# First key and value weights requested beside the feature tile that uses them, and modulation rows of 128 columns instead of 256

## The chip, the cores and the metric

One core of one Trainium2 chip runs the whole program. The metric is the device time of one execution in microseconds. The profile names the engines PE (TensorE: the matmuls), PEld (its weight loads), DVE (VectorE), ACT (ScalarE), POOL (GpSimd) and SP (SyncE, whose queue here issues all DMAs).

## What is computed

Two layers of a diffusion backbone over 1024 latent tokens and 256 context tokens, 1024 features wide. Each layer modulates its input with a per-feature shift and scale, projects it to queries, keys, values and a gate, attends, projects back, and ends in a LayerNorm. The change lies in the opening of the first layer, which is this part of the reference:

```python
shift, scale, gate = jnp.split(silu_c @ w_ada[i] + b_ada[i], 3, axis=-1)          # latent tokens
shift_c, scale_c, gate_c = jnp.split(silu_cc @ w_ada[i] + b_ada[i], 3, axis=-1)   # context tokens
u = h * (1.0 + scale[:, None, :]) + shift[:, None, :]
uc = hc * (1.0 + scale_c) + shift_c
...
q, k, v, g = _split_a(u @ w_in)      # 1024 queries, 256 keys, 256 values, 1024 gates
```

The rest of the first layer is windowed attention with four key and value heads, that of the second a neighbourhood attention. Neither is touched.

## The kernel before

Features lie on the 128 partitions: the input is eight feature tiles (`kt` = 0 to 7) of 128 features by 1280 tokens, cut into three chunks of 512, 512 and 256 tokens. Keys and values of the first layer need the sum over all eight feature tiles, and the kernel builds them while the tiles arrive. For each `kt` it does this:

- `mod_load`: two requests for the modulation weights (`wada`, 512 KB each, the halves `hf` of the contracted dimension) and one for the input tile (`hraw`, 640 KB). `Weights.load(n)` requests the first n of eight key and value weight pieces (`wr`, 256 KB each; pieces 0, 1, 4, 5 are keys, 2, 3, 6, 7 values; key pieces serve four feature tiles, value pieces two).
- `mod_rows` (line 503): matmuls of the 32-column `sil` (SiLU of the conditioning; two of its 32 columns are used) with `wada`, into four strips of 32 partitions of the PSUM tile `kc`, and a copy of the strips to SBUF by ACT (`rows`, line 505). Each strip holds a partial sum over a quarter of the features, for 256 columns: 128 of shift, 128 of scale.
- `mod` (line 512): a matmul of `rows` with the 0/1 matrix `sel` adds the four partial sums and turns them into columns, and DVE adds the bias (`adc`, line 513).
- `u_make` (lines 527 to 532): ACT scales and shifts chunk 0, DVE chunks 1 and 2; ACT rounds to a high part `uAh`, DVE subtracts for a low part `uAl`.
- `Weights.split(n)`: the same high and low split for weight pieces: ACT's cast (line 160, `wh` for keys, `wv` for values), DVE's subtraction (line 162).
- `k_mm` (lines 541 to 543): 12 matmuls of 512 columns into four key accumulators (`kp`), and six of 256 columns into `kc`. `v_mm` (lines 551 to 553): 12 matmuls of 256 columns into `vps`.

So a chain runs from `wada`'s landing through line 503, the copy, line 512, `adc` and `u_make` to the key and value matmuls of the same tile. The matmuls named `warm` and `vps<-zero` (line 446) compute nothing that is kept.

The code states the work per tile in a loop; a scheduler then fixes the order on each engine, and each engine runs its own list in that order, waiting on semaphores. SP issues its requests in order too, and the list of SP has eight semaphores in turn, so a request waits until the one eight places ahead has landed. A request into a buffer also waits until the buffer's last reader is done: `wr` has four buffers in this stage, `hraw` four, and `wada` shares ten with the split value weights. Since `kc` is one tile, the six key matmuls into it wait for the ACT copy out of it. The stage ends at the first matmul named `pv`, line 240, the values of the remaining tokens.

Of the kernel before, what the change touches and what calls it, by code (L numbers as in the profile page):

```python
# [11 lines left out]
F32 = mybir.dt.float32  # L12
# [7 lines left out]
P = 128  # L20
# [60 lines left out]
def build(tc, i, out):  # L81
    nc = tc.nc
    mm = nc.tensor.matmul
# [3 lines left out]
    def pool(name, side="left", **kw):  # L87
        st = ExitStack()
        p = st.enter_context(tc.tile_pool(name=name, bufs=1, side=side, reuse_waits="tile", **kw))
        return p, st  # L90
# [4 lines left out]
    def psbig(name):  # L95
        return ps.tile([P, 1024], F32, tag="big", bufs=2, name=name)
# [4 lines left out]
    cp = es.enter_context(tc.tile_pool(name="cp", bufs=1, side="left"))  # L101
    ident = cp.tile([P, P], F32, name="ident")
    cT = cp.tile([P, KT, 2], F32, name="cT")
    dma(cT, i["cT"])
    bad = cp.tile([P, 50], F32, name="bad")
    dma(bad, i["bada"])
    sel = bad[:, 48:50]
    lnc = cp.tile([P, 2, KT], F32, name="lnc")
    half = cp.tile([P, 1], F32, name="half")
    nc.vector.memset(half, -0.5)  # L110
# [75 lines left out]
    w = Weights(srcs)  # L186
# [247 lines left out]
    pp, pp_st = pool("p0", "right")  # L434
# [3 lines left out]
    sil = pp.tile([P, KT, 32], F32, name="sil")  # L438
# [5 lines left out]
    def warm(out, n):  # L444
        for _ in range(n):
            mm(out, zero[:, 0:P], zero, start=True, stop=True)
# [40 lines left out]
    kc = psbig("kc")  # L487
    vps = psbig("vps")
    raws, wada, rows = {}, {}, {}

    def mod_load(kt):
        wada[kt] = [pp.tile([P, 4, 2 * P], F32, tag="wada", bufs=10, name="wada") for _ in range(2)]
        for hf in range(2):
            dma(wada[kt][hf], i["wadaC"][kt, hf])
        raws[kt] = pp.tile([P, T], F32, tag="hraw", bufs=4, name="hraw")
        dma(raws[kt], i["hT"][:, kt, :])

    def mod_rows(kt):

        for hf, wt in enumerate(wada.pop(kt)):  # L500
            for g in range(4):
                gs = slice(32 * g, 32 * g + 32)
                mm(kc[gs, 512:768], sil[:, 4 * hf + g, :], wt[:, g, :], start=hf == 0, stop=hf == 1, tile_position=(0, 32 * g))
        rows[kt] = pp.tile([P, 2 * P], F32, tag="rows", bufs=2, name="rows")
        nc.scalar.copy(rows[kt], kc[:, 512:768])

    def mod(kt):

        r = rows.pop(kt)
        pa = kc[:, 768 + 4 * kt : 772 + 4 * kt]  # L510
        for x in range(2):
            mm(pa[:, 2 * x : 2 * x + 2], r[:, x * P : (x + 1) * P], sel, start=True, stop=True)
        nc.vector.tensor_tensor(
            adc[:, kt],
            pa.rearrange("p (x v) -> p x v", x=2),
            bad[:, kt : kt + 9 : 8].unsqueeze(2).to_broadcast([P, 2, 2]),
            ALU.add,
        )

    def u_make(kt):  # L520
        r = raws.pop(kt)
        for c, (t0, n) in enumerate(CHUNKS):
            v, tok = c // 2, slice(t0, t0 + n)
            x = r[:, tok]
            sc, sh = adc[:, kt, 1, v : v + 1], adc[:, kt, 0, v : v + 1]
            if c == 0:
                nc.scalar.activation(x, x, AF.Identity, bias=sh, scale=sc)
            else:
                nc.vector.tensor_scalar(x, x, sc, sh, ALU.mult, ALU.add)
            hi, lo = uA.at(kt, tok)  # L530
            nc.scalar.copy(hi, x)
            nc.vector.tensor_tensor(lo, x, f32(hi), ALU.subtract)

    def k_mm(kt):
        for c, (t0, n) in enumerate(CHUNKS):
            for nt in range(2):
                hi, lo = w.got[KEYS[2 * (kt // 4) + nt]]
                sl = slice((kt % 4) * P, (kt % 4 + 1) * P)
                rh, rl = uA.at(kt, slice(t0, t0 + n))
                pt = kps[c, nt] if c < 2 else kc[:, nt * C : nt * C + C]  # L540
                mm(pt, hi[:, sl], rh, start=kt == 0 and (c < 2 or nt == 0), stop=False)
                mm(pt, lo[:, sl], rh, start=False, stop=False)
                mm(pt, hi[:, sl], rl, start=False, stop=kt == KT - 1 and (c < 2 or nt == 1))

    def v_mm(kt):
        hi, lo = w.got[VALUES[kt // 2]]
        sl = slice((kt % 2) * 256, (kt % 2 + 1) * 256)
        for t in range(4):
            lh, ll = uA.at(kt, slice(t * P, (t + 1) * P))
            pt = vps[:, t * 256 : (t + 1) * 256]  # L550
            mm(pt, lh, hi[:, sl], start=kt == 0 and t % 2 == 0, stop=False)
            mm(pt, lh, lo[:, sl], start=False, stop=False)
            mm(pt, ll, hi[:, sl], start=False, stop=kt == KT - 1 and t % 2 == 1)


    upto = (3, 4, 6, 7, 8)
    for kt in range(-1, KT + 1):
        if kt + 1 < KT:
            for n in range(3) if kt < 0 else (kt + 3,) if kt + 3 < KT else ():
                mod_load(n)  # L560
                w.load(upto[min(n, 4)])
            mod_rows(kt + 1)
        if kt > 0:
            k_mm(kt - 1)
        if kt + 1 < KT:
            mod(kt + 1)
        if kt < 0:

            warm(vps[:, 0:512], 8)
        if kt > 0:  # L570
            v_mm(kt - 1)
        if kt < KT and kt >= 0:
            u_make(kt)
            w.split(upto[min(kt, 4)])
    dma(ident, i["ident"])
    dma(lnc, i["lnc"])
    dma(cos, i["cos"])
# [224 lines left out]
    for p in range(8):  # L802
# [6 lines left out]
        if p < 7:  # L809
            n = len(att)  # L810
# [72 lines left out]
    for b in range(10):  # L883
# [14 lines left out]
        g = gts[:, b // 8]  # L898
# [229 lines left out]
    for n, row in enumerate(rowsB):  # L1128
        ex = []
        if n < len(subsB):  # L1130
            h, jp, r = subsB[n]
# [55 lines left out]
    for b in range(8):  # L1187
        x = ob.tile([P, D], F32, tag="x", bufs=2, name="x")
# [130 lines left out]
```

## Time and profile before

| | |
|---|---|
| times of three runs | 1464.61, 1461.41 and 1463.99 us, median 1463.99 |
| profiled execution | 1466.38 us, of which the span is 1464.6 us |
| mean granted clock of TensorE over the span | 0.992 |
| TensorE busy | 1399.2 us, 96% of the span |
| stage of the change | from the start to the first `pv` matmul at 72.92 us |

A row of the timeline gives the start in us, the length, the engine, line, operation, tiles and the number of instructions merged into the row; in square brackets stands the idle time of that engine before it, and whose work ended it. Several rows of TensorE overlap, since a matmul starts while the one ahead is still flowing through the array; from one start to the next is what a matmul costs. A row of the table by windows gives the stretch, its length, for PE, PEld, DVE, ACT and POOL the busy time and the number of instructions (x), and then the granted clock of TensorE, the busy share of the DMA engines and GB/s. Of the DMA answers, the last number of a row is the time from the issue to the landing.

### The profile page before, as it was taken

The numbers are of one execution on the slowest core, as the hardware profiler recorded it, in microseconds if no ns is written. First come the engines' busy times: TensorE is split into PE (matmuls) and PEld (weight loads), VectorE is DVE, ScalarE is ACT, GpSimd is POOL, SyncE is SP. The second block draws the span as 40 slices with busy tenths as digits, with TensorE's granted clock in tenths as the row PEclk, the third lists the DMA queues.
The fourth block names the chain that finished last, engine by engine and source line by source line (L and its number), as shares of the span: only waits on it lengthen the run. The fifth ranks groups of instructions, "written<-read, shape, count | busy, mean of one in ns | idle before, by whom it ended". The sixth has DMA issues, their size and how long they took to land.

```text
span 1464.6 us, 24919 instructions
## 1 busy us (share of the span) xinstructions
PE 1399.2 (96%) x8700; PEld 1216.0 (83%) x8700; DVE 989.2 (68%) x2220; ACT 734.7 (50%) x1565; POOL 631.1 (43%) x779
## 2 busy tenths in 40 slices
PE   8999999999999999999999999999999999988995
PEld 4797888888888888788898889888988898877784
DVE  3567888878788789566432765555565656577788
ACT  3436677676676778332222544544454444466300
POOL 0136767666576657233211323333233323355664
PEclk9999999999999999999999999999999999999998
DMA  7564114122222114344277564454555465563543
GB/s 285 207 213 122 51 62 120 52 86 80 80 69 62 62 53 133 128 134 138 71 229 221 159 177 153 132 173 140 172 144 175 119 187 141 146 191 108 145 114 92
DMA packets 117228, 195.03 MB, mean 133 GB/s; under 512 B 9328, under 2 KB 57840, under 8 KB 117104
## 3 DMA queue, kind: packets, MB, share of 16 engines
q1 hardware_dynamic: 117104, 193.45, 43.6%
q8 instruction: 69, 1.13, 0.3%
q14 instruction: 55, 0.45, 0.1%
HBM read 141.51 MB, written 51.90 MB: 132 GB/s over the span
## 4 chain that ended last, share of the span: by engine, by line
PE 70%; DVE 11%; DMA 5%; issue 5%; ACT 4%; POOL 3%; SPq 0%; DVEq 0%; ACTq 0%; POOLq 0%
PE pj L207 9%; PE pj L208 8%; PE pj L206 8%; PE T_B L334 4%; PE T_A L334 4%; PE pvB L1058 3%; PE pvA L725 3%; PE S_A L696 2%; PE pv L240 2%; PE pv L242 2%; PE pv L241 2%; PE S_B L1027 2%; DMA gwB<-in_wadaT 2%; PE yA L419 2%; PE yA L418 2%
## 5 line engine op out<-in xcount | busy, mean ns | idle before, releaser
L327 POOL TENSOR_SCALAR s_B<-s_B,rs_B 128x640 f32<-128x640 f32 (+1 forms) x128 | 102.5, 801 | 310.5 <-DVE rs_B L326 288.2
L206 PE MATMUL pj<-uBh,wh 128*128 128x512 f32 (+1 forms) x448 | 176.6, 394 | 0.0
L207 PE MATMUL pj<-uBl,wh 128*128 128x512 f32 (+1 forms) x448 | 170.5, 381 | 0.0
L208 PE MATMUL pj<-uBh,wl 128*128 128x512 f32 (+1 forms) x448 | 170.3, 380 | 0.0
L322 ACT ACTIVATE s_B<-s_B,m_B 128x640 f32<-128x640 f32 (+1 forms) x128 | 102.9, 804 | 123.2 <-DVE m_B L315 122.2
L322 ACT ACTIVATE s_A<-s_A,m_A 128x641 f32<-128x641 f32 (+2 forms) x160 | 119.5, 747 | 89.0 <-DVE m_A L315 73.7
L340 DVE TENSOR_TENSOR pt_B<-T_B,pt_B 128x640 fp32r<-128x640 f32 (+1 forms) x128 | 100.9, 788 | 80.5 <-ACT pt_B L338 79.9
L162 POOL TENSOR_TENSOR wl<-wr,wh 128x512 fp32r<-128x512 f32 x64 | 87.1, 1362 | 156.5 <-ACT wh L160 152.5
L327 POOL TENSOR_SCALAR s_A<-s_A,rs_A 128x640 f32<-128x640 f32 (+2 forms) x160 | 126.8, 793 | 58.5 <-DVE rs_A L326 56.4
L315 DVE CUSTOM_DVE_ANT_0 s_A<-S_A,msk,nsk 128x640 f32<-128x640 f32 (+2 forms) x160 | 123.5, 774 | 34.0 <-PE S_A L697 17.8
L206 PE MATMUL pj<-uAh,wh 128*128 128x512 f32 (+1 forms) x384 | 140.0, 365 | 0.0
L207 PE MATMUL pj<-uAl,wh 128*128 128x512 f32 (+1 forms) x384 | 137.7, 358 | 0.0
L208 PE MATMUL pj<-uAh,wl 128*128 128x512 f32 (+1 forms) x384 | 137.3, 358 | 0.0
L340 DVE TENSOR_TENSOR ptl_A<-T_A,pth_A 128x640 fp32r<-128x640 f32 (+2 forms) x160 | 113.9, 712 | 15.2 <-PE pvA L725 7.4
L338 ACT CAST pt_B<-T_B 128x640 fp32r<-128x640 f32 (+1 forms) x128 | 84.4, 659 | 65.9 <-PE T_B L334 65.3
L334 PE MATMUL T_A<-ident,s_A 128*128 128x128 f32 x672 | 101.0, 275 | 12.4 <-DVE m_A L315 8.8
L334 PEld LDWEIGHTS T_A<-ident,s_A 128*128 128x128 f32 x672 | 77.2, 140 | 40.3 <-issue 17.5
L315 DVE CUSTOM_DVE_ANT_0 s_B<-S_B,bias 128x640 f32<-128x640 f32 (+1 forms) x128 | 100.3, 784 | 10.8 <-PE S_B L1028 9.9
L338 ACT CAST pth_A<-T_A 128x640 fp32r<-128x640 f32 (+2 forms) x160 | 96.4, 603 | 16.7 <-PE T_A L334 14.0
L334 PE MATMUL T_B<-ident,s_B 128*128 128x128 f32 x608 | 88.2, 274 | 13.8 <-DVE pt_B L340 9.4
L208 PEld LDWEIGHTS pj<-uBh,wl 128*128 128x128 f32 x448 | 84.5, 189 | 17.0
L334 PEld LDWEIGHTS T_B<-ident,s_B 128*128 128x128 f32 x608 | 70.0, 140 | 31.2 <-issue 12.5
(219 smaller groups left out, 3904.4 us busy)
## 6 DMA issues: line engine op xcount, KB each, us to landing
kB<-kdB SPq DMA_DIRECT2D x64, 320.0 KB, 5.3
gw<-in_wadaT SPq DMA_DIRECT2D x48, 256.0 KB, 2.8
vdB<-st SPq DMA_DIRECT2D x20, 512.0 KB, 3.1
vB<-vdB SPq DMA_DIRECT2D x16, 640.0 KB, 4.7
wada<-in_wadaC SPq DMA_DIRECT2D x16, 512.0 KB, 8.2
kdB<-st SPq DMA_DIRECT2D x16, 512.0 KB, 2.8
qdB<-st SPq DMA_DIRECT2D x16, 512.0 KB, 3.6
qB<-qdB SPq DMA_DIRECT2D x32, 256.0 KB, 4.6
```

What stands on the lines that cost most here:

```text
L162: e.tensor_tensor(lo, r, f32(hi), ALU.subtract)
L206: mm(pt[:, :n], hi[:, sl], rh, start=kt == 0, stop=False)
L207: mm(pt[:, :n], hi[:, sl], rl, start=False, stop=False)
L208: mm(pt[:, :n], lo[:, sl], rh, start=False, stop=kt == KT - 1)
L315: nc.vector.tensor_tensor_reduce(outp, sc, in1, scale, init if init is not None else 3e38, ALU.add, ALU.min, accum_out=s.m)
L322: nc.scalar.activation(s.t[:, :n], s.t[:, :n], AF.Exp, bias=s.m, scale=-1.0, accum_out=s.sum)
L327: nc.gpsimd.tensor_scalar(s.t[:, : s.w], s.t[:, : s.w], s.rs, 1.0, ALU.mult, ALU.mult)
L334: nc.tensor.transpose(tp[:, k * P : (k + 1) * P], s.t[:, src * P : (src + 1) * P], ident)
L338: nc.scalar.copy(pt.hi[:, :n, hl, :], tv)
L340: nc.vector.tensor_tensor(pt.lo[:, :n, hl, :], tv, f32(pt.hi[:, :n, hl, :]), ALU.subtract)
L725: mm(o, vA[p // 2][:, t, :], x, start=k == 0 and not part, stop=part == 1 and k == len(tl) - 1)
L1058: mm(ov[:, :, 1], v[:, t, :], x[:, k], start=not side and k + n == 0, stop=k == 3 and n == 1)
```

## The change

Requests: key pieces 0 and 1 are asked for between the first tile's `wada` and its `hraw`, value piece 2 between those of the second tile, value piece 3 between those of the third; pieces 4 and 5 come with the fifth tile, 6 with the sixth, 7 with the seventh. Splits are called for earlier: pieces 0 and 1 with the first load, and later ones a tile ahead of their use. The rows: a matmul of line 503 now takes 128 columns instead of 256, shift to strips 0 and 1 and scale to strips 2 and 3, so there are twice as many, half as long; `rows` is 128 wide, and one matmul with a four-column `sel` does what two did. There are 12 instead of eight `vps<-zero` matmuls.

```diff
-    sel = bad[:, 48:50]
+    sel = bad[:, 48:52]
...
-    def mod_load(kt):
+    def mod_load(kt, upto):
         wada[kt] = [pp.tile([P, 4, 2 * P], F32, tag="wada", bufs=10, name="wada") for _ in range(2)]
         for hf in range(2):
             dma(wada[kt][hf], i["wadaC"][kt, hf])
+        w.load(upto)
         raws[kt] = pp.tile([P, T], F32, tag="hraw", bufs=4, name="hraw")
         dma(raws[kt], i["hT"][:, kt, :])
...
-            for g in range(4):
-                gs = slice(32 * g, 32 * g + 32)
-                mm(kc[gs, 512:768], sil[:, 4 * hf + g, :], wt[:, g, :], start=hf == 0, stop=hf == 1, tile_position=(0, 32 * g))
-        rows[kt] = pp.tile([P, 2 * P], F32, tag="rows", bufs=2, name="rows")
-        nc.scalar.copy(rows[kt], kc[:, 512:768])
+            for r in range(2):
+                for x in range(2):
+                    for kh in range(2):
+                        g = 32 * (2 * x + kh)
+                        mm(
+                            kc[g : g + 32, 512:640], sil[:, 4 * hf + 2 * r + kh, :], wt[:, 2 * r + kh, x * P : (x + 1) * P],
+                            start=hf + r == 0, stop=hf + r == 2, tile_position=(0, g),
+                        )
+        rows[kt] = pp.tile([P, P], F32, tag="rows", bufs=2, name="rows")
+        nc.scalar.copy(rows[kt], kc[:, 512:640])
...
-        for x in range(2):
-            mm(pa[:, 2 * x : 2 * x + 2], r[:, x * P : (x + 1) * P], sel, start=True, stop=True)
+        mm(pa, rows.pop(kt), sel, start=True, stop=True)
...
-    upto = (3, 4, 6, 7, 8)
+    upto = (2, 3, 4, 4, 6, 7, 8, 8)
...
-                mod_load(n)
-                w.load(upto[min(n, 4)])
+                mod_load(n, upto[n])
+                if n == 0:
+                    w.split(2)
...
-            warm(vps[:, 0:512], 8)
+            warm(vps[:, 0:512], 12)
...
-            w.split(upto[min(kt, 4)])
+            w.split(upto[min(kt + 1, 7)])
```

The scheduler's order changes with it on every engine up to the end of this stage; after it each engine's list reads as before. Three places matter. The first is SP's list from the first `wada` request. Before:

```order
L494 DMA wada<-in_wadaC 128x1024 x2
L496 DMA hraw<-in_hT 128x1280
L146 DMA wr_156<-in_wAk 128x512
L146 DMA wr_158<-in_wAk 128x512
L146 DMA wr_160<-in_wAv 128x512
L494 DMA wada<-in_wadaC 128x1024 x2
L496 DMA hraw<-in_hT 128x1280
L146 DMA wr_168<-in_wAv 128x512
L494 DMA wada<-in_wadaC 128x1024 x2
L496 DMA hraw<-in_hT 128x1280
L146 DMA wr_176<-in_wAk 128x512
L146 DMA wr_178<-in_wAk 128x512
```

And in the changed kernel, where the numbers behind `wr` differ but the sources after the arrow are the same:

```order
L495 DMA wada<-in_wadaC 128x1024 x2
L146 DMA wr_154<-in_wAk 128x512
L146 DMA wr_156<-in_wAk 128x512
L498 DMA hraw<-in_hT 128x1280
L495 DMA wada<-in_wadaC 128x1024 x2
L146 DMA wr_172<-in_wAv 128x512
L498 DMA hraw<-in_hT 128x1280
L495 DMA wada<-in_wadaC 128x1024 x2
L146 DMA wr_180<-in_wAv 128x512
L498 DMA hraw<-in_hT 128x1280
L495 DMA wada<-in_wadaC 128x1024 x2
L498 DMA hraw<-in_hT 128x1280
```

Two key pieces moved ahead of the first input tile, one value piece from ahead of the second `wada` pair to behind it, and the second pair of key pieces from ahead of the fourth `wada` pair to behind the fifth.

The second place is PE's list around the second `mod` (line 512 before, 517 after), which releases the second feature tile. `kp_0` and `kp_1` are the key accumulators, `uAh`/`uAl` the tile's high and low parts, `wh`/`wl` those of a key piece. Before:

```order
L543 MATMUL kp_0_146<-uAl_109,wh_231 128x512
L541 MATMUL kp_1_147<-uAh_106,wh_235 128x512
L503 MATMUL kc<-wada,sil 32x256 x4
L542 MATMUL kp_1_147<-uAh_106,wl_236 128x512
L543 MATMUL kp_1_147<-uAl_109,wh_235 128x512
L512 MATMUL kc<-bad,rows 128x2 x2
L541 MATMUL kp_0_146<-uAh_106,wh_231 128x512
```

After (lines 546 to 548 are the former 541 to 543):

```order
L547 MATMUL kp_1_145<-uAh_105,wl_165 128x512
L507 MATMUL kc<-wada,sil 32x128 x8
L548 MATMUL kp_1_145<-uAl_108,wh_164 128x512
L546 MATMUL kp_0_146<-uAh_106,wh_160 128x512
L517 MATMUL kc<-bad,rows 128x4
L547 MATMUL kp_0_146<-uAh_106,wl_161 128x512
L548 MATMUL kp_0_146<-uAl_109,wh_160 128x512
L546 MATMUL kp_1_147<-uAh_106,wh_164 128x512
L547 MATMUL kp_1_147<-uAh_106,wl_165 128x512
L548 MATMUL kp_1_147<-uAl_109,wh_164 128x512
L546 MATMUL kp_0_146<-uAh_106,wh_160 128x512
```

The last row of each piece is the first matmul of the second feature tile: before, it stands right behind `mod`; now five matmuls of the first tile stand between. The first of this tile's two row groups, which stood behind five `kp` matmuls, now stands ahead of all of them.

The third place is PE's list behind the third `mod`. Before, the next matmul is the third tile's own:

```order
L543 MATMUL kc<-uAl_110,wh_235 128x256
L512 MATMUL kc<-bad,rows 128x2 x2
L541 MATMUL kp_0_146<-uAh_106,wh_231 128x512
L542 MATMUL kp_0_146<-uAh_106,wl_232 128x512
L541 MATMUL kp_1_147<-uAh_106,wh_235 128x512
```

After, four key matmuls of the second tile and the first tile's 12 value matmuls (`vps`, lines 556 to 558, formerly 551 to 553; two of them are shown) follow it:

```order
L548 MATMUL kc<-uAl_110,wh_164 128x256
L517 MATMUL kc<-bad,rows 128x4
L548 MATMUL kp_0_146<-uAl_109,wh_160 128x512
L546 MATMUL kp_1_147<-uAh_106,wh_164 128x512
L547 MATMUL kp_1_147<-uAh_106,wl_165 128x512
L548 MATMUL kp_1_147<-uAl_109,wh_164 128x512
L556 MATMUL vps<-wv_251,uAh_105 128x256
L557 MATMUL vps<-wv_251,uAh_105 128x256
```

They use value piece 2, whose cast on ACT moved from behind the third tile's first two `uAh` casts to ahead of that tile's `u_make`; its DVE subtraction stands behind the third tile's two `hraw` operations.

More of the change, by code (lines that the diff above doesn't have):

```diff
@@ L104, in build @@
     dma(cT, i["cT"])
-    bad = cp.tile([P, 50], F32, name="bad")
+    bad = cp.tile([P, 52], F32, name="bad")
     dma(bad, i["bada"])
-    sel = bad[:, 48:50]
+    sel = bad[:, 48:52]
     lnc = cp.tile([P, 2, KT], F32, name="lnc")
@@ L500, in mod_rows @@
         for hf, wt in enumerate(wada.pop(kt)):
-            for g in range(4):
-                gs = slice(32 * g, 32 * g + 32)
-                mm(kc[gs, 512:768], sil[:, 4 * hf + g, :], wt[:, g, :], start=hf == 0, stop=hf == 1, tile_position=(0, 32 * g))
-        rows[kt] = pp.tile([P, 2 * P], F32, tag="rows", bufs=2, name="rows")
-        nc.scalar.copy(rows[kt], kc[:, 512:768])
+            for r in range(2):
[8 more added lines that the diff above has]
+        nc.scalar.copy(rows[kt], kc[:, 512:640])
     def mod(kt):
-        r = rows.pop(kt)
         pa = kc[:, 768 + 4 * kt : 772 + 4 * kt]
-        for x in range(2):
-            mm(pa[:, 2 * x : 2 * x + 2], r[:, x * P : (x + 1) * P], sel, start=True, stop=True)
+        mm(pa, rows.pop(kt), sel, start=True, stop=True)
         nc.vector.tensor_tensor(
@@ L1277 @@
     rel = np.zeros((NH, 32, 31), np.float32)
-    sel = np.tile(np.eye(32, 2, dtype=np.float32), (4, 1))
+    sel = np.kron(np.eye(2, dtype=np.float32), np.tile(np.eye(32, 2, dtype=np.float32), (2, 1)))
     rel[:, 8:23] = b_rel_bias[0][:, ::-1, ::-1]
```

## The prediction

> **What bounds the kernel now.** I read the page first, to see which engine the end waits for.
>
> ```profile
> span 1464.6 us, 24919 instructions
> PE 1399.2 (96%) x8700; PEld 1216.0 (83%) x8700; DVE 989.2 (68%) x2220; ACT 734.7 (50%) x1565; POOL 631.1 (43%) x779
> ```
>
> TensorE is busy 96% of the span, so a microsecond saved in the opening stage is kept only if TensorE saves it. The order behind the stage is unchanged, and its first matmul depends on the stage's last, so a gain at the stage's end should move everything behind it. That end is here:
>
> ```profile
> 72.92 0.28 PE L240 MATMUL pv-1_2_738<-wv,uAh 128*128 128x256 f32 x1
> ```
>
> Next the table by windows, over the stretches in which the granted clock was constant:
>
> ```profile
> 8.56:11.98 3.42, 0.85 (x6) 0.35 (x6) 2.46 (x6) 2.79 (x6) 0.00 (x0) 1.00 1.05 421
> 11.98:15.39 3.41, 3.41 (x13) 1.56 (x13) 1.40 (x3) 0.40 (x1) 0.00 (x0) 0.50 1.02 408
> 18.80:22.22 3.42, 1.99 (x14) 1.09 (x14) 2.51 (x6) 2.15 (x4) 0.00 (x0) 1.00 1.04 405
> 25.63:29.05 3.42, 1.74 (x10) 1.44 (x11) 2.46 (x6) 2.79 (x6) 0.00 (x0) 1.00 0.00 0
> 29.05:32.46 3.41, 3.41 (x13) 1.95 (x12) 2.00 (x4) 0.92 (x2) 0.00 (x0) 0.50 0.52 185
> 32.46:72.92 40.46, 40.46 (x295) 31.89 (x295) 19.92 (x41) 15.38 (x31) 4.55 (x4) 1.00 0.58 222
> ```
>
> TensorE idles in three of these (busy 0.85, 1.99 and 1.74 us of 3.42). After the first and the third the clock is 0.50 for 3.41 us: half the work, so 1.7 us lost each time. After the one with 1.99 us it stays at 1.00. From 32.46 us on TensorE has no idle time: there only its own work counts. DMA stood still from 25.63 to 29.05 (0 GB/s).
>
> Then the timeline around the idle time. For the first tile:
>
> ```profile
> 9.19 0.81 ACT L527 ACTIVATE hraw<-hraw,adc 128x512 f32<-128x512 f32 x1 [0.96 <-DVE adc L513]
> 9.91 1.43 ACT L531 CAST uAh<-hraw 128x512 fp32r<-128x512 f32 x3
> 11.91 1.74 PE L541 MATMUL kp<-uAh,wh 128*128 128x512 f32 x3 [2.57 <-ACT wh L160]
> 12.10 1.28 DVE L162 TENSOR_TENSOR wl<-wr,wh 128x512 fp32r<-128x512 f32 x2
> ```
>
> For the second and the third:
>
> ```profile
> 17.95 0.60 PE L512 MATMUL kc<-bad,rows 128*128 128x2 f32 x4
> 18.66 0.16 DVE L513 TENSOR_TENSOR adc<-kc,bad 128x4 f32<-128x4 f32 x1 [5.28 <-PE kc L512]
> 18.85 0.87 DVE L529 TENSOR_SCALAR hraw<-hraw,adc 128x512 f32<-128x512 f32 x2
> 20.23 0.50 PE L541 MATMUL kp<-uAh,wh 128*128 128x512 f32 x1 [1.68 <-ACT uAh L531]
> 25.46 0.50 PE L512 MATMUL kc<-bad,rows 128*128 128x2 f32 x4
> 26.07 0.16 DVE L513 TENSOR_TENSOR adc<-kc,bad 128x4 f32<-128x4 f32 x1 [4.24 <-PE kc L512]
> 27.64 0.50 PE L541 MATMUL kp<-uAh,wh 128*128 128x512 f32 x1 [1.68 <-ACT uAh L531]
> 28.83 0.69 DVE L162 TENSOR_TENSOR wv<-wr,wv 128x512 fp32r<-128x512 f32 x1
> ```
>
> Both times TensorE finishes `mod` and has nothing to do until its own result has come back as `uAh`: 2.28 and 2.18 us from the start of `mod` to the next matmul. The first tile's value matmuls could have filled the second hole, but their split came at 28.83.
>
> **Prices.** A key matmul of 512 columns and a value matmul of 256, from start to start, and the groups as the chain of waits lists them:
>
> ```profile
> 43.68 0.39 PE L541 MATMUL kp<-uAh,wh 128*128 128x512 f32 x1
> 43.91 0.39 PE L542 MATMUL kp<-uAh,wl 128*128 128x512 f32 x1
> 46.42 0.28 PE L553 MATMUL vps<-wv,uAl 128*128 128x256 f32 x1
> 46.54 0.28 PE L551 MATMUL vps<-wv,uAh 128*128 128x256 f32 x1
> 14.51 1.01 PE kc L503 x8
> 51.88 0.57 PE kc L503 x8
> 49.59 0.34 PE kc L512 x4
> ```
>
> So 0.23 us, 0.12 us, 0.57 us for half a tile's rows at full clock (1.01 at half clock) and 0.34 for a `mod`.
>
> **The change, part by part.**
>
> *Requests.* SP's issues, and the time to landing of the first `hraw`, the second key piece, the second tile's first `wada` half and its `hraw`, each from the DMA answer for the window of its issue:
>
> ```profile
> 2.59 0.43 SPq L496 DMA_DIRECT2D hraw<-in_hT  x1
> 3.07 0.96 SPq L146 DMA_DIRECT2D wr<-in_wAk  x2
> 4.57 0.93 SPq L494 DMA_DIRECT2D wada<-in_wadaC  x2
> 5.54 0.55 SPq L496 DMA_DIRECT2D hraw<-in_hT  x1
> hraw<-in_hT SPq DMA_DIRECT2D x1, 640.0 KB, 5.9
> wr<-in_wAk SPq DMA_DIRECT2D x1, 256.0 KB, 6.2
> wada<-in_wadaC SPq DMA_DIRECT2D x1, 512.0 KB, 7.2
> hraw<-in_hT SPq DMA_DIRECT2D x1, 640.0 KB, 9.1
> ```
>
> The first `hraw` landed at 2.59 + 5.9 = 8.5, the second key piece (issued 3.55) at 9.75, the second tile's first `wada` half at 11.8. Now the key pieces come first, so by the same bytes `hraw` lands at about 9.7; `u_make` starts at 9.8 instead of 9.19. In return the two weight casts and DVE's 1.28 us of subtractions lie ahead of it. From `u_make`'s start, the second `uAh` cast is done after 0.72 + 1.2 = 1.9 us: first key matmul at 11.8, or 12.2 if DVE's subtractions delay chunk 1 by 0.4. Against 11.91 that costs -0.1 to +0.3; I take +0.1. The second tile's `wada` has one 256 KB piece less ahead of it (0.6 us at the 421 GB/s of its window) and lands at 11.2, so its first half of rows runs in the hole ahead of 11.9: 0.57 to 1.01 us off the path; I take 0.7, since it was paid at half clock.
>
> SP stood from its issue at 15.29 to 29.54, because a value piece wanted a buffer that the late value split held:
>
> ```profile
> 15.29 0.33 SPq L496 DMA_DIRECT2D hraw<-in_hT  x1
> 29.54 0.33 SPq L146 DMA_DIRECT2D wr<-in_wAv  x1
> ```
>
> That goes, but by itself it is worth nothing: TensorE never waited on a landing there. At 0.4 MB/us (408 GB/s in the table) four tiles of 1.7 MB with four pieces, 7.9 MB, take 20 us and all eight with eight pieces, 15.7 MB, 39 us; the first bytes move at about 3, so the fourth tile's input lands near 23 and the last near 42, each ahead of its use.
>
> *The second tile's hole, 1.68 us.* Five key matmuls stand behind `mod` now: 5 x 0.23 = 1.15, and `mod` is 0.17 shorter. The way from `mod`'s start to the next matmul, 2.28 before (0.60 of `mod` and 1.68 idle), becomes 2.11, of which 0.43 is `mod` and 1.15 key matmuls: 0.5 to 0.7 us stay idle. Saved: 1.0. Its `hraw` landed at 14.6 in this trace (5.54 + 9.1) and `adc` is now due at about 14.9, so this is tight; late by 1 us, it costs that.
>
> *The third tile's hole, 1.68.* Four key and 12 value matmuls follow `mod`, 4 x 0.23 + 12 x 0.12 = 2.4 us. But value piece 2 is subtracted on DVE behind `adc` (0.16) and two `hraw` operations (0.87 for the pair at 18.85), so 0.69 us of subtraction ends about 1.8 us after `adc` starts, and TensorE reaches it after some 0.9. Late next: `wv`'s low part, 0.9 idle. Saved: 0.8.
>
> *The clock.* With these holes at 0.7 and 0.9 us, and 8.56 to 11.98 filled by more warm matmuls and the early half of rows (2.3 of 3.42 us, above the 1.99 that kept the clock), neither half-clock stretch should come: 2 x 1.7 = 3.4. Ends 0 and 3.4.
>
> *The half-wide rows.* `mod` has one matmul instead of two: half of 0.34, 0.17 for each of the seven tiles in the busy part: 1.2. The copy on ACT gets shorter, which lies on the path only in the two holes above. In line 507 the columns are the same, 2 x 128 instead of 256, with twice the weight loads. Are the loads hidden?
>
> ```profile
> 33.12 1.06 PE L503 MATMUL kc<-wada,sil 128*32 128x256 f32 x14
> 33.36 0.12 PEld L503 LDWEIGHTS kc<-wada,sil 128*32 128x32 f32 x3
> ```
>
> The 14 matmuls run through from 33.12, and three loads for the same strips, 0.11 each, fall inside at 33.36. A wave of four strips streams 0.57 / 2, less a drain, some 0.22; at 128 columns 0.11, about as long as a load. So I take +0.03 per half and 14 halves: +0.4. If no load were hidden, four waves would pay 0.11 each: +0.44 per half, +6.2 in all. Ends 0 and 6.2; I take the low one, by the row of the loads.
>
> The Trainium skill speaks against this: its page "TensorE: Matmul & The Clock Gate" says in Part 3 that a weight load overlaps running matmuls only where their row groups differ, and these all use every row. By it the rows would cost 6.2 us more. The trace disagrees: the loads at 33.36 do overlap.
>
> *Sum:* -1.0 - 0.8 - 3.4 - 1.2 - 0.7 + 0.1 + 0.4 = -6.6 us, against the profiled execution: 1466.4 to 1459.8. That execution was 2.4 us above the median of the runs, 1463.99. If the median run has the same two half-clock stretches, it becomes 1457.4; if it has one, 1459.1. I take 1457.9.
>
> The same page of the Trainium skill, "TensorE: Matmul & The Clock Gate", says in Part 1 that the clock falls only after an idle window of about 3.4 us, and that the windows run freely, not from the kernel's start. The first half disagrees with these rows (1.74 busy of 3.42 was enough); no run here shows the second. If it holds, runs of the kernel before differ in how many stretches they catch.
>
> **Rivals.**
>
> *The clock was not to be had.* The runs of before catch none or one stretch, or the changed kernel keeps one. For it: they spread over 3.2 us, about two stretches. Against it: the profiled run caught both. Gain 3.2 to 4.9: 1459.1 to 1460.8. This is still faster.
>
> *Weight loads show.* At +0.44 per half, the gain of 6.6 loses the other 5.8: 1463.2, no change.
>
> *The strips run one after the other.* If the eight short matmuls of a half no longer share the array, the place is line 507, the price 8 x 0.17 (a short matmul pair of `mod`, 0.34 / 2) = 1.36 instead of 0.57, +0.8 per half and +11 in all: 1469, slower. It decides from +0.7 per half. Against it: in the row at 33.12, 14 matmuls take 0.99 us to the next one's start, so four strips do share.
>
> *A late input.* If `hraw` or `wada` of the second or third tile slips by 1 us in the new queue, each hole grows by as much and half-clock stretches return: 1459 to 1463.
>
> **How the numbers follow.** Forecast (gain above 5 us): 0.55. Clock not to be had, or a late input of up to 1 us (gain 3 to 5): 0.24. Weight loads or late inputs eat it: 0.15. Strips one after another: 0.06. The runs differ by 0.2%, about 2.9 us, without any change; that is what a measurement can tell. Faster needs less than 1461.06: 0.55 + 0.24, and a little of the third, 0.80; same 0.13, slower 0.07. The range reaches up to 1461.4, into the third case, and down to 1454.8: all of 6.6 from the median, no idle left (another 1.6) and half of the noise, 1.
>
> **What the changed profile would show.** First `pv` matmul at 66 to 67 instead of 72.9; clock 1.00 from 12 to 66; idle rows of 0.5 to 0.9 ahead of the second tile's first `kp` matmul and of the second `vps` row; rows of x16 in 0.55 to 0.65 us at line 507; no stop of SP between 15 and 29 us. Groups at line 507 of 1 us would prove the weight loads right. A stage that ends 6 us earlier with the whole unchanged would prove that something behind it gives the time back, for which the trace has no sign.

## The result, and the profile after

The changed kernel took 1452.84 us in the median of four executions (1450.12 to 1453.81), the kernel before 1463.20 beside it (1461.41 to 1464.61): ratio 0.9919, 95% interval [0.9902, 0.9936], a gain of 9.4 to 14.3 us. The forecast of 1457.9 had the direction; the time lies 2 us below its range.

The profiled execution took 1452.42 us, 14.0 less than the one before. The page's first lines, and from the timeline the first rows and the stage's end:

```profile
span 1450.4 us, 25150 instructions
PE 1392.4 (96%) x8816; PEld 1214.8 (84%) x8816; DVE 991.1 (68%) x2220; ACT 733.6 (51%) x1565; POOL 632.2 (44%) x779
6.42 0.32 PE L507 MATMUL kc<-wada,sil 128*32 128x128 f32 x4
64.62 0.28 PE L240 MATMUL pv-1_2_798<-wv,uAh 128*128 128x256 f32 x1
```

TensorE's busy time fell by 6.8 us (from 1399.2) and its idle time by 7.4 (from 65.4, the span less the busy time). The stage ends 8.3 us sooner (64.62 against 72.92), although the first rows began 0.6 later, at 6.42 instead of 5.83. They stand behind 12 warm matmuls; before, and then in the changed kernel:

```profile
1.21 4.69 PE L446 MATMUL warm<-zero 128*128 128x512 bf16 x12 [1.21 <-DVE zero L442]
5.83 0.64 PE L503 MATMUL kc<-wada,sil 128*32 128x256 f32 x8
```

```profile
1.21 5.29 PE L446 MATMUL warm<-zero 128*128 128x512 bf16 x12 [1.21 <-DVE zero L442]
```

One warm matmul follows the other by 0.43 us until the first full-clock window begins, at 5.15 us in the one execution and at 6.34 in the other, and by 0.22 after that. Over the 18 profiles that window began between 3.91 and 7.19 us, and the rows the later the later it came, between 5.2 and 6.4, so their start is no effect of the change. So below "the stage" is counted from the first rows' matmul to the first `pv` matmul: 67.09 us before, 58.20 after.

The table by windows over the stage, cut where the earlier one was cut: at the clock's own boundaries (busy time and count of PE, PEld, DVE, ACT, POOL, then the granted clock, DMA share, GB/s):

```profile
9.76:13.17 3.41, 2.35 (x25) 1.12 (x23) 2.97 (x7) 2.15 (x5) 0.00 (x0) 1.00 1.03 420
13.17:16.58 3.41, 3.33 (x28) 2.03 (x27) 1.28 (x4) 1.38 (x3) 0.00 (x0) 1.00 1.01 406
20.00:23.41 3.41, 2.76 (x20) 2.11 (x15) 1.66 (x5) 2.29 (x5) 0.00 (x0) 1.00 1.02 410
26.82:64.62 37.80, 37.80 (x331) 31.49 (x331) 21.23 (x43) 15.06 (x32) 4.56 (x4) 1.00 0.58 224
```

No window is less than 2.35 us busy, and the clock stays at 1.00. In the second and third profile of the changed kernel (below) the lowest window was busy for less, and the clock stayed up there too:

```profile
8.14:11.55 3.41, 1.77 (x11) 0.71 (x12) 2.34 (x5) 2.25 (x5) 0.00 (x0) 1.00 1.01 407
7.98:11.39 3.41, 1.88 (x14) 0.82 (x16) 2.36 (x6) 2.36 (x5) 0.00 (x0) 1.00 1.01 409
```

The idle time ahead of the key and value matmuls of the first three tiles stands in the first, third and fourth of these rows of the timeline; the second is the first key matmul:

```profile
11.75 0.65 PE L507 MATMUL kc<-wada,sil 128*32 128x128 f32 x16 [1.06 <-DMA wada<-in_wadaC]
12.34 0.50 PE L546 MATMUL kp<-uAh,wh 128*128 128x512 f32 x1
16.84 0.51 PE L546 MATMUL kp<-uAh,wh 128*128 128x512 f32 x1 [0.34 <-ACT uAh L536]
23.44 0.39 PE L557 MATMUL vps<-wv,uAh 128*128 128x256 f32 x1 [0.68 <-DVE wv L162]
```

And the prices: from the chain of waits a half tile's rows, now eight short matmuls; from the timeline a `mod` and the matmul behind it. Each fp32 matmul leaves a pair of records, so eight are x16 and one is x2:

```profile
36.88 0.57 PE kc L507 x16
33.46 0.28 PE L517 MATMUL kc<-bad,rows 128*128 128x4 f32 x2
33.60 0.37 PE L556 MATMUL vps<-wv,uAh 128*128 128x256 f32 x1
```

The rows cost 0.57 as before, `mod` 33.60 - 33.46 = 0.14 instead of 0.34 in the chain.

### The profile page after: what moved, and what is told of

It is laid out like the page before. It is cut to its first block, busy times and chain, and to the rows that moved or that the text cites. A ratio compares the mean times of both kernels' runs of the same rounds, so it can differ in the third digit from the quotient of the medians.

```text
span 1450.4 us, 25150 instructions
## 1 busy us (share of the span) xinstructions
PE 1392.4 (96%) x8816; PEld 1214.8 (84%) x8816; DVE 991.1 (68%) x2220; ACT 733.6 (51%) x1565; POOL 632.2 (44%) x779
## 4 chain that ended last, share of the span: by engine, by line
PE 72%; DVE 11%; DMA 5%; issue 5%; ACT 4%; POOL 3%; SPq 0%; DVEq 0%; ACTq 0%; POOLq 0%
PE pj L207 9%; PE pj L206 9%; PE pj L208 9%; PE T_B L334 4%; PE T_A L334 4%; PE pvB L1064 3%; PE pvA L731 3%; PE pv L240 3%; PE pv L241 3%; PE pv L242 3%; PE S_A L702 2%; PE S_B L1033 2%; PE yA L419 2%; PE yA L418 2%; PE yA L417 2%
## 5 line engine op out<-in xcount | busy, mean ns | idle before, releaser
L334 PEld LDWEIGHTS T_B<-ident,s_B 128*128 128x128 f32 x608 | 70.0, 140 | 29.8 <-issue 11.8
```

Source lines behind the costliest of these rows:

```text
L334: nc.tensor.transpose(tp[:, k * P : (k + 1) * P], s.t[:, src * P : (src + 1) * P], ident)
```

## The experiments

Four groups of four kernels ran, each group on one chip, on four different chips, with executions of the kernel before among them (medians 1466.07, 1465.03, 1463.59 and 1463.55). "Late" are half-clock stretches behind 100 us. The clock is the mean over all executions of the mean granted clock of each, which is given to 0.001; a stretch of 3.41 us at half clock lowers it by 0.0012, and the tail of the kernel alone, where TensorE is done, leaves 0.995 to 0.996.

| kernel | ratio to before | median us | stage us | half-clock stretches in its profile | clock |
|---|---|---|---|---|---|
| before, 62 executions | | 1463.5 to 1466.1 | 67.09, 67.40 | 2 + 1 late; 2 | 0.9926 |
| changed, first | 0.9919 | 1452.84 | 58.20 | 0 | 0.9955 |
| rows only | 0.9955 | 1459.74 | 63.96 | 2 | 0.9927 |
| requests only | 0.9959 | 1460.74 | 62.34 | 1 + 2 late | 0.9930 |
| before, holes filled | 0.9948, 0.9974 | 1458.53, 1460.76 | 64.31, 64.25 | 0, 0 | 0.9952 |
| changed, again | 0.9907, 0.9915 | 1452.06, 1452.49 | 58.54, 58.31 | 0, 0 | 0.9953 |
| requests, 12 warm | 0.9964, 0.9954 | 1459.84, 1456.66 | 60.78, 60.92 | 1 late, 0 | 0.9944, 0.9960 |
| changed, 2 warm | 0.9943 | 1457.99 | 60.74 | 2 + 1 late | 0.9928 |
| changed, early split | 0.9911 | 1452.49 | 58.62 | 0 | 0.9952 |
| changed, 28 warm | 0.9966 | 1458.40 | 59.17 | 0 | 0.9952 |
| changed, wide buffer | 0.9927 | 1452.01 | 58.12 | 1 late | 0.9946 |
| rows only, holes filled | 0.9941 | 1454.53 | 61.06 | 0 | 0.9954 |
| changed, rows x3 | 0.9921 | 1453.45 | 60.08 | 0 | 0.9953 |
| changed, rows x5 | 0.9938 | 1454.93 | 60.97 | 2 late | 0.9943 |

The intervals of the ratios reach 0.0012 to 0.0019 to each side, 2 to 3 us. Behind the stage every engine's list of instructions is the same in all these kernels but the last two.

**First group: each half of the change, the clock alone, and nothing.** Rows only is the kernel before with the change's lines 501 to 517 (per tile 16 short matmuls, a copy of 128, one `mod` matmul).

> The kernel before with the half-wide rows alone (matmuls of 128 columns, one matmul in mod, a copy of 128 columns); requests, splits and the eight warm matmuls as before. Theory A (the requests' new order fills the two holes of 1.68 us and keeps the clock at 1.00; the rows give little): both holes stay at 1.5 to 1.7 us, so one or both half-clock stretches stay; from mod alone 7 x 0.22 = 1.6 us, with fewer half-clock stretches up to 5: first pv matmul at 68 to 71 us (before 72.9), total 2 to 5 us below the kernel before. Theory B (the shorter rows shorten each tile's chain and carry most of the gain): 6 us or more, first pv at 66.5 or earlier. Theory C (part of the gain is made behind the stage): the total falls by some 2 to 4 us more than the first pv matmul moves.

Requests only has the other edits of the diff, but eight warm matmuls and wide rows as before.

> The changed kernel with the rows of 256 columns, the two matmuls in mod and the eight warm matmuls back; requests and splits as changed. Theory A: holes of 0.8 and 1.2 us in place of 1.68, clock 1.00 but perhaps for one stretch; first pv matmul at 67 to 68.5 us, total 4.5 to 6 us below the kernel before. Theory B: holes of 1.5 us, 3 us or less below. Theory C: as for the rows alone, the total falls by 2 to 4 us more than the first pv matmul moves.

Holes filled is the kernel before plus matmuls that are not kept (six more ahead of the first key matmul, and three behind the second and the third `mod`):

```diff
+        for _ in range(3 if kt in (1, 2) else 0):
+            mm(vps[:, 0:256], r[:, 0:P], r, start=True, stop=True)
...
-            warm(vps[:, 0:512], 8)
+            warm(vps[:, 0:512], 14)
```

> The kernel before, with TensorE kept busy and nothing else: 14 warm matmuls instead of eight ahead of the first key matmul, and three matmuls of the rows with themselves (results not used) behind the second and the third mod, about 1.3 us in each hole. Requests and rows as before. If the half-clock stretches come from the holes (theory A): clock 1.00 from the warm-up on, first pv matmul 3 to 3.5 us earlier than the 72.9 of the profiled run, total 1.7 to 3.4 below the kernel before, as often as that has one or two stretches. If the stretches have another cause: they stay, and the total is the same or up to 0.5 us above.

> The kernel before, unchanged, for the spread between its executions. If the half-clock stretches of the first profile are the rule: the same two, first pv at 72.9, and the time between 1462 and 1466. If they are chance: none or one, first pv at 69.5 to 71.2, time nearer 1461 to 1463. Theory C's places behind the stage (the DMA waits of the second layer's start at 778 to 812 us, the half-clock stretch at 858 to 862) differ between the two profiles of this same kernel if they are chance, by about as much as they differ from the changed kernel's.

Unchanged, the kernel before gave 0.9993 [0.9981, 1.0006]. Its profile had the two early half-clock stretches again, from 12.30 and 29.37 us, and none near 858. Rows only gave 0.9955 [0.9939, 0.9970] and requests only 0.9959 [0.9944, 0.9975]: 6.6 and 6.0 us, so each half brings about half of the whole, and neither keeps the clock. The stage was shorter by 3.1 to 3.4 us with rows only and by 4.8 to 5.1 with requests only; the rest of the two gains, 3.2 to 3.5 and 0.9 to 1.3 us, lies outside the stage, as Theory C had it, or in the spread. Windows of rows only, then of requests only:

```profile
10.24:13.65 3.41, 1.32 (x5) 0.85 (x5) 2.92 (x6) 2.53 (x6) 0.00 (x0) 1.00 1.02 417
13.65:17.07 3.42, 3.42 (x22) 1.76 (x20) 0.12 (x1) 0.00 (x0) 0.00 (x0) 0.50 1.05 413
17.07:20.48 3.41, 2.13 (x23) 1.39 (x23) 1.35 (x4) 1.93 (x4) 0.00 (x0) 1.00 1.02 397
20.48:23.89 3.41, 3.41 (x22) 2.08 (x22) 1.32 (x3) 0.48 (x2) 0.00 (x0) 0.50 0.99 396
```

```profile
10.50:13.91 3.41, 1.57 (x12) 0.80 (x13) 3.05 (x7) 2.19 (x4) 0.00 (x0) 1.00 1.03 415
13.91:17.33 3.42, 3.42 (x15) 1.67 (x15) 0.16 (x1) 0.37 (x1) 0.00 (x0) 0.50 1.03 412
850.18:853.59 3.41, 1.29 (x8) 0.82 (x6) 2.20 (x5) 0.00 (x0) 0.00 (x0) 1.00 0.62 183
853.59:857.01 3.42, 3.39 (x12) 3.13 (x13) 2.13 (x6) 2.12 (x4) 0.84 (x2) 0.50 0.59 216
```

Filling the holes left the chain as long as before and kept the clock up; the windows that were its lowest:

```profile
9.62:13.03 3.41, 2.11 (x10) 0.74 (x7) 2.88 (x7) 3.19 (x6) 0.00 (x0) 1.00 1.04 425
16.45:19.86 3.41, 3.13 (x18) 2.20 (x15) 1.49 (x4) 2.18 (x5) 0.00 (x0) 1.00 1.03 404
```

It gained 7.6 us (0.9948 [0.9931, 0.9966]); repeated in the fourth group it gained 3.8 (0.9974 [0.9961, 0.9987]). Both are more than the 1.7 to 3.4 that I expected at first. The stage was shorter by 2.8 to 3.2 us in both. The mean clock on the two chips rose by 0.0036 and 0.0020, which is 3.0 and 1.7 stretches or 5.1 and 2.8 us; the 2.5 and 1.0 us beyond that no run here explains. The two values also show how badly such a number repeats.

**Second group: the clock in the changed kernel.** The changed kernel again; the requests with 12 warm matmuls and wide rows (the change without its rows); the changed kernel with two warm matmuls instead of 12; and one with value piece 2 split a tile earlier, to take away the wait at 23.44:

```diff
-                if n == 0:
-                    w.split(2)
+                if n < 2:
+                    w.split(2 + n)
```

> The changed kernel unchanged, on the chip of the next three. Theory: no execution catches a half-clock stretch, so the mean granted clock is 0.995 or 0.996 in each, while those of the kernel before spread from 0.989 to 0.995. Median 1451 to 1454 us, ratio 0.990 to 0.993; first pv matmul at 64 to 65.5 us. Rival (the first measurement of the change was a lucky set of executions): some of its executions at 0.993 or less, median 1455 to 1457, ratio 0.994 to 0.996.

> The changed kernel with wide rows and two mod matmuls again (the other way round: requests alone, but with 12 warm matmuls instead of eight). Theory: the warm matmuls keep the clock at 1.00 from about 6 us on, so what is missing against the changed kernel is the price of the rows alone: 7 x 0.22 us for mod, and 0.1 to 0.4 in each of two holes, 1.7 to 2.4 us: median 1454.5 to 1455.5, first pv matmul at 66.3 to 67, no half-clock stretch in the profile. Rival 1 (the rows themselves are worth what rows alone measured, 5 to 6 us): 1458 to 1459. Rival 2 (the warm matmuls don't matter, the late half-clock stretches belong to the wide rows): as requests alone, 1460 to 1461, with a half-clock stretch near 14.

> The changed kernel with two warm matmuls instead of 12 ahead of the first key matmul. Theory: the window between about 8 and 13 us falls below half busy, and a half-clock stretch of 3.41 us follows; it costs 1.7 us less what of it falls into the holes ahead of the second and third tile's key matmuls (0.34 and 0.68 us): 0.7 to 1.7, so median 1453.5 to 1454.5, mean clock 0.994 or so, first pv matmul at 65.3 to 66.3. Rival (the order of the requests alone keeps the clock): clock 0.995, median as the changed kernel's.

> The changed kernel with value piece 2 split a tile earlier, so that the first tile's value matmuls run behind the second tile's mod and the second tile's wait of 0.68 us for wv ahead of the third tile's goes. Theory: what is left to save in this stage is the sum of its idle time, 0.34 + 0.68, and the wv subtraction of 0.69 now stands ahead of the second tile's hraw on DVE, covered by 12 value matmuls of 0.12: gain 0.3 to 1.0, median 1451.5 to 1452.5. Rival (DVE and ACT become the chain of the second tile): the uAh of the second tile comes 0.6 to 0.7 us later, and the gain is zero or a loss of up to 0.5.

The change repeated: 0.9907 [0.9890, 0.9925], and no execution below 0.995. With two warm matmuls the clock went, for two windows in a row, and 0.9943 [0.9925, 0.9961] was left:

```profile
7.32:10.73 3.41, 0.82 (x18) 0.46 (x10) 2.08 (x5) 2.01 (x4) 0.00 (x0) 1.00 1.03 414
10.73:14.14 3.41, 2.79 (x34) 1.59 (x34) 1.79 (x4) 1.44 (x4) 0.00 (x0) 0.50 1.03 418
14.14:17.56 3.42, 3.42 (x13) 2.77 (x10) 1.86 (x5) 2.42 (x5) 0.00 (x0) 0.50 1.04 411
```

That is the warm matmuls' worth, 5.9 us, where I had expected 0.7 to 1.7 for ten of them: the stage grew by 2.2, and a late stretch came into the profiled execution and, by the clock of 0.992, into others. Requests with 12 warm matmuls kept the early clock, and their stage was 2.2 to 2.6 us longer than the changed kernel's, as the price of the rows had it; the whole was 7.8 longer, with a late stretch in its profile and, by a clock of 0.994, in about eight of 12 executions:

```profile
728.50:731.91 3.41, 1.81 (x14) 1.58 (x13) 1.77 (x8) 0.62 (x1) 0.00 (x0) 1.00 0.96 323
731.91:735.32 3.41, 3.41 (x19) 3.41 (x17) 0.23 (x2) 0.00 (x0) 0.00 (x0) 0.50 0.95 260
```

So the stage nearly fits the theory (1.7 to 2.4), and the whole lies 0.8 above the first rival's range; the next groups ask why. The four warm matmuls that the change adds took 1.6 us off the stage here (62.34 with requests only), yet the ratio is 0.9964 against 0.9959: in the whole no gain shows. The early split removed the wait for `wv`, but its subtraction now stands ahead of the second tile's `hraw`, and the third tile's `adc` came 0.7 later. In this kernel, and then in the changed one:

```profile
22.42 0.16 DVE L518 TENSOR_TENSOR adc<-kc,bad 128x4 f32<-128x4 f32 x1 [3.45 <-PE kc L517]
```

```profile
21.71 0.16 DVE L518 TENSOR_TENSOR adc<-kc,bad 128x4 f32<-128x4 f32 x1 [3.27 <-PE kc L517]
```

No gain: 0.9911 against 0.9907, as its rival had it.

**Third group: is it the place in memory, and what does a later end cost?** 28 warm matmuls instead of 12 in the changed kernel; a wide buffer of which half is used; rows only with filled holes (14 warm matmuls, six of 128 columns behind the second and third `mod`); and the requests with 12 warm matmuls, with two more unused columns in the table of biases.

```diff
-            warm(vps[:, 0:512], 12)
+            warm(vps[:, 0:512], 28)
```

> The changed kernel with 28 warm matmuls instead of 12 ahead of the first key matmul: the stage ends later by pure work at full clock, 16 x 0.24 = 3.8 us less the 1.1 to 1.6 us that TensorE stood idle there, and the other engines' lists stay as they are. It tells how much of a later stage end arrives at the end. Theory (whole shift, nothing more): first pv matmul at 66.3 to 67.3 us, clock 0.995 to 0.996, median 1454.0 to 1455.5. Rival (what lies behind the stage depends on when the stage ends: the two kernels of the call before whose stage ended 1.8 and 2.3 us later took 6 to 8 us longer): 1457 to 1460, with half-clock stretches behind 700 us in most executions.

> The changed kernel, but its rows lie in a buffer of 256 columns, of which 128 are used: every engine's list is the same, only the places in memory of what is allocated behind it move. Theory: nothing depends on the place, 1451 to 1454 us. Rival (part of the gain of the half-wide rows is the place in memory of later tiles): 1455 to 1459.

> Half-wide rows alone, with the idle time ahead of the first three tiles' key matmuls filled by matmuls that are not kept (14 warm ones, and six of 128 columns behind the second and third mod), so that the clock stays up: against the kernel before with filled holes (1458.5) the clock is the same and only the rows differ. Theory: 7 x 0.22 = 1.5 us and up to 0.5 from the shorter chain: median 1456.5 to 1457.5, first pv matmul at 68.6 to 69.4. Rival (the rows are worth what rows alone gave, 5 to 6 us): 1452.5 to 1453.5.

> Requests with 12 warm matmuls and wide rows as before, with the table of biases padded from 50 to 52 columns as in the changed kernel; every engine's list is the same as without the padding. Theory: as without it, 1458.5 to 1460.5, with one half-clock stretch behind 700 us in most executions (clock 0.994). Rival (its place in memory, or an unlucky set of executions): the stage ends 2.3 us after that of the changed kernel, and so does the whole: 1454 to 1455.5, clock 0.995 to 0.996.

The buffer's place does nothing (1452.01). Rows with filled holes were 3.2 us shorter in the stage than filled holes alone, and in the whole 0.9941 against 0.9948 and 0.9974, 1 to 5 us: by the stage the rows' own worth, without the clock, is about 3 us, more than the 1.5 to 2 expected and less than the rival's 5 to 6. The requests with 12 warm matmuls came to 1456.66 here, between the theory and the rival: 4.7 over the wide buffer beside them, of which the stage holds 2.8. Their clock was 0.996 in all five executions, so the late stretch that they had without the padding, and on another chip, did not come; which of the two kept it away is not shown. 28 warm matmuls lengthened the stage by only 0.6 to 1.0 in the profiled execution, which took 1454.54, but the other four took 1457.6 to 1459.5 at a clock of 0.995 to 0.996. Neither the theory's time nor the rival's half-clock stretches came, and no profile shows what held those four up.

**Fourth group: does the stage's end arrive one to one?** The sixth tile's rows are computed three and five times, in the part where TensorE never waits; beside them the change and the filled holes again.

```diff
-        for hf, wt in enumerate(wada.pop(kt)):
+        for hf, wt in list(enumerate(wada.pop(kt))) * (3 if kt == 5 else 1):
```

> The changed kernel once more, beside the next three on the same chip. Theory: median 1450 to 1454 us, clock 0.995 or 0.996 in nearly all executions. Rival (the 13 us of the call before last was that chip): ratio 0.994 to 0.996.

> The changed kernel with the sixth tile's rows computed three times: four more groups of 16 short matmuls of 0.57 us, 2.3 us of pure work, in the part of the stage where TensorE never waits; the scheduler moves a few instructions near them and a few behind the stage. Theory (the stage's end is worth itself): 2.0 to 2.6 us more than the changed kernel, first pv matmul at 66.2 to 67.2, clock 0.995. Rival (a later end of the stage is paid two or three times, as 28 warm matmuls seemed to be): 5 to 7 us more.

> The same with the rows computed five times, 4.6 us of pure work. Theory: 4.2 to 5.0 us more than the changed kernel, first pv matmul at 68.4 to 69.4. Rival: 8 us or more.

> The kernel before with its idle time filled, once more, on the chip of the changed kernel. Theory: the clock alone is worth two to three stretches of 1.7 us, so 3.4 to 5.1 us less than the kernel before; the other 6 to 8 us to the changed kernel are the chain and the matmuls of the stage. Rival (of the 11 us most is the clock): within 3 us of the changed kernel.

The change gave 0.9915 [0.9896, 0.9934], with a clock of 0.994 in two of six executions. Against it the stage grew by 1.8 and 2.7 us (the added groups ran in 0.46 each, back to back, less than the 0.57 I had put), and the medians by 1.0 and 2.4. With intervals of 2 us or more that does not fix the share, but a stage that is paid two or three times, the rival, would have given 3.6 to 8 us and falls. These two kernels have another order in a few places behind the stage, and near 129 us TensorE waits for 2.1 us in them, where the others have a wait of 1.3; the first of the second kernel's late stretches follows that wait. Its other one shows what else moves the whole. The profile of the second (two windows, then two rows of its timeline):

```profile
730.16:733.57 3.41, 0.72 (x6) 0.65 (x5) 0.72 (x2) 0.62 (x1) 0.00 (x0) 1.00 0.94 329
733.57:736.98 3.41, 3.41 (x18) 3.38 (x17) 1.19 (x6) 0.00 (x0) 0.00 (x0) 0.50 0.63 195
...
732.87 0.50 PE L240 MATMUL pv<-wh,uBh 128*128 128x256 f32 x2 [2.69 <-ACT wh L160]
...
732.20 0.62 ACT L160 CAST wh<-wr 128x512 fp32r<-128x512 f32 x1 [3.75 <-DMA wr<-in_wBv]
```

At this place in the second layer TensorE waits for a weight piece. In the changed kernel the same row says:

```profile
727.39 0.39 PE L240 MATMUL pv<-wh,uBh 128*128 128x256 f32 x1 [1.28 <-ACT wh L160]
```

Over the profiles of all these kernels this wait lasts from 0.4 to 3.1 us, and behind it stand the stretches near 730 us of four profiles. All idle time of TensorE between 64 and 1432 us, added up over the rows, is 37.4 to 41.6 us: 41.4 and 40.3 in the two profiles of the kernel before, 38.2, 40.2 and 38.6 in the three of the changed one.

## Why the prediction fell short

*What was right.* The direction, and the third tile's next wait by name (`wv`'s low part). SP no longer stands for 14 us between 15 and 29 us. Neither early half-clock stretch came in any of the three profiles; by the filled holes that is 2.8 to 3.2 us of the stage, where the sum had 3.4. The 2.3 us of busy time that were to keep the clock came true by where the window lay in the first profile: in the two others the window was busy for 1.77 and 1.88 us, and the clock of other kernels fell after such windows.

*The step that failed: the sum, "-1.0 - 0.8 - 3.4 - 1.2 - 0.7 + 0.1 + 0.4 = -6.6".* The stage fell by 8.9 us (67.09 to 58.20). The clock's term was a little too large; the others, which add up to -3.2, were together half of what came. The kernel before with its holes filled has the old chain and the full clock, so the difference between it and the changed kernel shows each of them. The times of the first profile of each are summed over the stage from one matmul's start to the next, in us, with idle time counted by itself:

| | the sum had | holes filled | changed | difference |
|---|---|---|---|---|
| idle time behind the first key matmul, and what fills it | -1.8 | 3.65 | 1.20 | -2.45 |
| seven `mod` | -1.2 | 2.63 | 0.98 | -1.65 |
| rows behind the first key matmul, 14 halves and 13 | -0.7 + 0.4 | 8.37 | 7.19 | -1.18 |
| from the first rows to the first key matmul | +0.1 | 6.09 | 5.92 | -0.17 |
| 48 matmuls into `kc`, 96 into `vps` | nothing | 18.98 | 18.06 | -0.92 |
| 96 matmuls into `kp` | nothing | 24.58 | 24.86 | +0.28 |
| together | -3.2 | 64.3 | 58.2 | -6.1 |

*Each term.* The second hole shrank to 0.34 us instead of 0.5 to 0.7, the third to 0.68 instead of 0.9; another 0.18 is a wait for `wada` at 19.47. `mod` saved 0.36 - 0.14 = 0.22 from start to start, not half of 0.34. The `kc` and `vps` matmuls the sum left out: a matmul of 256 columns takes 0.12 where it follows its like, and 19 of the 144 took more than 0.17 with filled holes, nine in the changed kernel. That fewer of them stand right behind rows or `mod` fits this; no run here tests it.

*The rows.* The weight loads are hidden: eight short matmuls cost 0.57. The sum had +0.4 for them, and over the 13 halves between the first key matmul and the first `pv` matmul it was 7.19 us against 7.12 for wide rows in the same order of requests: +0.1. The rule that the Trainium skill gives in Part 3 of "TensorE: Matmul & The Clock Gate" (a load overlaps only where row groups differ) would have made it 0.44 a half, 5.7 us; the trace disagrees. The strips share the array as before. Against the filled holes the rows fell by more than the half that left (0.57), because there one half is split, and its first matmul alone takes 0.55.

*The input.* It was later than the forecast: `u_make` began at 10.44 instead of 9.8, and TensorE waited for the second tile's `wada` until 11.75 instead of 11.2. That cost about half a microsecond. The first `uAh` was there at 11.79, when the DVE operation that waits for it began:

```profile
11.79 1.63 DVE L537 TENSOR_TENSOR uAl<-hraw,uAh 128x512 fp32r<-128x512 f32 x3 [0.44 <-ACT uAh L536]
```

But the rows stood ahead of the first key matmul until 12.34, 0.1 behind the forecast's 11.8 to 12.2. So this half of rows, the -0.7 of the sum, did not run in a hole after all. The two other profiles show the same order of events. It is the rival of a late input, at about half of its 1 us.

*The step from the stage to the whole.* "A gain at the stage's end should move everything behind it": the repeated rows do not speak against it, but the tables that I read stopped at 72.92. The profiled execution before had a third half-clock stretch, behind a wait in the second layer:

```profile
855.07:858.48 3.41, 1.20 (x8) 0.80 (x7) 2.83 (x6) 0.18 (x1) 0.00 (x0) 1.00 0.63 194
858.48:861.90 3.42, 3.42 (x11) 2.94 (x10) 2.69 (x7) 2.13 (x5) 1.86 (x2) 0.50 0.57 206
```

The execution after had none, which is 1.7 us, and 3.1 us less waiting between 64 and 1432. Most of that is the spread between executions: from the first `pv` matmul to the end it is 1392 and 1387 us in the two profiles before, 1386, 1388 and 1387 in the three of the changed kernel. So of the 14.0 us between the first two profiles, some 4 belong to the execution that was caught.

*From the profiled execution to the median.* "If the median run has the same two half-clock stretches, it becomes 1457.4; if it has one, 1459.1. I take 1457.9." That gave 0.5 us away by letting the median execution have fewer stretches than the profiled one. The 62 executions of the kernel before have a mean clock of 0.9926, from 0.989 to 0.995, and the profiled one had 0.992, so it was an ordinary one. The rival "the clock was not to be had" took the spread of three runs for a sign of fewer stretches; of the 62 executions 37 have a higher clock than 0.992, but none is above 0.995, and 17 have a lower one.

*The account.* Means over all executions: 1465.0 before, 1452.4 after, 12.6 less. The stage without the clock is 6 of that. The mean clock rose from 0.9926 to 0.9953 over the changed kernel's 16 executions, 2.3 stretches: at 1.7 us each that is 3.9. Within the kernel before the mean time falls only from 1468.8 us at 0.989 to 1463.2 at 0.995, 1.1 us a stretch, which would make it 2.5. The last 2.7 to 4.1 are not settled: they lie behind the stage or in the difference of chips; the filled holes repeated only to 3.8 us, and two kernels (28 warm matmuls, requests with 12) took 2 to 5 us longer than their stages and clocks account for. The wait near 730 us varies by as much, but why more of that should fall on one kernel than on another no run here shows.

## What to carry to other kernels

A hole on TensorE costs twice where it halves the clock of what follows (here 1.7 us idle, then 1.7 lost): before shortening a chain, fill its holes with matmuls that are not kept and see what the clock alone gives. Read the windows of the whole profile, not of the stage of the change, and the granted clock of every execution, since the profiled one holds one draw of how many stretches are caught. The two halves of this change gain 6 us each where the whole gains 10 to 13, so it was not one mechanism: count each term from start to start over the whole stage, including the matmuls that the change does not touch.

## What the runs showed of the hardware

- The windows after which the clock changes are 3.413 us long and lie differently in the executions of one kernel: in the three profiles of the changed kernel the first full-clock window began at 6.34, 4.73 and 4.56 us, and over all 18 profiles anywhere from 3.91 to 7.19. This shows the second half of what the Trainium skill says in Part 1 of "TensorE: Matmul & The Clock Gate" (the windows run freely).
- A window need not be idle for the clock to fall. Of the windows at full clock up to 1425 us in the 18 profiles, all ten with less than 1.5 us of busy time were followed by half clock, none with more than 2.2. Between 1.5 and 2.14 us six were, the busiest at 2.13 in rows only, and 101 were not, among them one of 1.55. So TensorE's busy time as the profile counts it is not quite the measure, and the 1.99 us that the prediction took as enough was no safe bound. And one window that was itself at half clock, 2.79 us busy, was followed by half clock again (two warm matmuls).
- Eight matmuls of 128 columns in four strips cost the same 0.57 us as four of 256, and in a longer uninterrupted run 0.46.
